# Fixed places for the backward fills and another order of heads in the paired DeltaNet scan

## The chip, the cores and the metric

One core of one Trainium2 chip. The time is the device time of one execution in microseconds (us); for before there are three runs and one profiled execution. An effect under about 0.2% (5 us) can't be told from no change here.

## What is computed

One layer of a hybrid backbone over 128 context tokens and 2048 latent tokens, width 1024. A normed and modulated input goes through one combined projection; half of its width feeds a gated DeltaNet with 4 heads of 128 in both directions, the other half a gated MLP; one output projection joins them, then comes a squared-ReLU MLP. The part that the change touches is the DeltaNet scan. Cut to its core:

```python
def step(S, xs):
    qd, kd, u_c, w_c, qk_c, gl = xs
    v_new = u_c - w_c @ S
    o = qd @ S + qk_c @ v_new
    S = S * exp(gl) + kd.T @ v_new
    return S, o
# u_c, w_c come from a triangular solve of (I + strict_lower(k_beta k^T * decay)) per chunk and head
out = concat([rmsnorm(o_f + flip(o_b)) * silu(gate), o_mlp]) @ w_out
```

## The kernel before

The program has three stages: the projections (up to about 457 us), the scan (457 to 1262 us), and the wide MLP. Instructions are issued in the order of a list of events, and the framework's scheduler then orders each engine's queue within the dependencies it is given. Every queue runs in order.

**Units and pairs.** The scan works on chunks of 128 tokens, `unit(t, d)` (d = 0 forward, 1 backward). There are 34 units, taken in pairs: the two context units first, then 16 forward units, then 16 backward ones. A pair inverts its two triangular matrices together, 8 heads at once (heads 0 to 3 are the first chunk's, 4 to 7 the second's), in fp16. These are the "prep" steps of `pair`: X is turned for each chunk (`turn`, L1143: four products on TensorE, then the copy Y on ScalarE); five levels, w = 2 to 32, each of two steps (`level`, L1157 to L1192); a last level at half size (L1206, L1218, L1222) and the refinement (L1234 to L1236) up to T (L1243, evicted by ScalarE at L1247). In a level the first step multiplies AH by Y for all heads (L1167), and VectorE copies the masked result into P (L1170); the second step multiplies P with X twice (L1181, L1187), and ScalarE copies the results back into Y and X (L1190). So a level goes TensorE, VectorE, TensorE, ScalarE, and each of these hands over to the next.

**The chain.** Each unit has four scan steps ("chain"): S by kT (L991) with vt on VectorE (L1049); vt by T (L991) with the copy vn on ScalarE (L1057); vn by kt (L991) with the new S on VectorE (L1079); and the output o (L1090, L1091; eviction L1094 to L1102). The next unit needs S.

**Fills.** Everything else in this stage is put between: the gMLP's projections while the forward units run, and in the backward part the output projection of finished tiles: gate and norm of o (L1385 to L1397), its transposes (`trans`, L1410), their two-part evictions oH on ScalarE (L1414) and oL on VectorE (L1415), 48 products per tile (L219 to L221), and the residual (L1434, L1435). For four of the tiles, operands of the MLP are prepared too (opH on ScalarE L873, opL on VectorE L874, stored by DMA L876).

**What sets the order.** Every event has a time in units of one chunk; `WINDOWS` (L57, L58) gives the windows: entries 2 and 3 are the chain's window of a unit, for forward (entries 0 to 7) and backward (8 to 17); entries 4 and 5 of the backward half are when norm, scaling and the two transposes of a unit are due, entries 6 and 7 its output projection, entries 8 and 9 the MLP's operands. `emit` adds ordering edges: a fill's first product on TensorE stands behind the newest chain or prep step but `lag`:

```python
elif pe and len(hist) > lag:
    tc.add_manual_dep(pe[0], hist[-1 - lag].name, ...)
for time, _, f, kind in sorted(events, key=lambda e: e[:2]):
    emit(f, kind, LAG2 if time < NT + 1 else LAG3)
```

`LAG2` is 0 and `LAG3` is 3. A three-product group L219, L220, L221 is one 128-row part of a product in split precision; a fill piece in this stage is two of them, six matmuls.

Of the kernel before, what the change touches and what calls it, by code (L numbers as in the profile page):

```python
# [24 lines left out]
H = 4  # L25
# [6 lines left out]
def interleave(*lists):  # L32
# [5 lines left out]
    for _, _, _, s in sorted(order, key=lambda e: e[:3]):  # L38
# [3 lines left out]
MOD_STEPS = (1, 1, 0, 0, 0, 1, 0, 2, 0, 1, 1, 2)  # L42
NS = 4
LAG2 = 0
LAG3 = 3
NF = 5
LATE = 0.1
PARTS = ((0, 2), (2, 4), (4, 6), (6, 8))
# [5 lines left out]
NK = DFF // P // 2  # L54
AHEAD = 3
COMPUTE = (mybir.EngineType.DVE, mybir.EngineType.Activation, mybir.EngineType.Pool)
WINDOWS = [2.0, 0.0, -0.225, 0.775, -2.1, 18.9, 17.58, 18.3,  # L57
           2.0, 0.0, -0.225, 0.775, 1.22, 1.5, 1.6875, 2.6875, 3.17, 3.71]  # L58


@with_exitstack
def hybrid_step(
# [7 lines left out]
    V, A, G, T = nc.vector, nc.scalar, nc.gpsimd, nc.tensor  # L70
# [12 lines left out]
    def f32(ap):  # L83
        return ap.bitcast(F32)
# [195 lines left out]
    with ExitStack() as ph:  # L280
# [478 lines left out]
        for bi in range(len(BLOCKS)):  # L759
# [8 lines left out]
            for n, (gi, h) in enumerate(order):  # L768
                u = us[n] if bi == 0 and n < 3 else feature_tile(blk, bi, gi, h)
# [156 lines left out]
    with ExitStack() as ph:  # L926
# [48 lines left out]
        def first_pe(fn):  # L975

            start = len(tc.nc.cur_bb.bb.instructions)
            fn()
            return [x.name for x in tc.nc.cur_bb.bb.instructions[start:] if x.engine == mybir.EngineType.PE][0]

        def unit(t, d, last=False):

            u = {}
# [5 lines left out]
            def quad(p, lhs, rhs):  # L989
                for h in range(H):  # L990
                    T.matmul(p[:, h, :], lhs[:, h, :], rhs[:, h, :], start=True, stop=True)  # L991
# [60 lines left out]
            @scan.append  # L1052
            def _():
                p = pd()
                pe = first_pe(lambda: quad(p, u["T"], u["vt"]))
                u["vn"] = q32("vn", 1)
                A.copy(u["vn"], p)  # L1057
                if not last:
                    behind(lambda: [A.activation(u["kt"][:, h, :], u["kt"][:, h, :], AF.Copy, scale=col(eglg, h))
                                    for h in range(H)], pe)  # L1060
                u["pe"] = pe
# [51 lines left out]
        def pair(us):  # L1113
# [3 lines left out]
            spans = [(0, 8, ds[0])] if ds[0] == ds[1] else [(0, 4, ds[0]), (4, 8, ds[1])]  # L1117
# [41 lines left out]
            def level(w):  # L1159

                @steps.append
                def _():
                    p = packed(pd8(), w)
                    for lo, hi, d in spans:
                        y = half(g["Y"], 1 - d, w)
                        for h in range(lo, hi):
                            T.matmul(p[:, h], g["AH"][:, h, :], y[:, h], start=True, stop=True)  # L1167
                    for lo, hi, d in spans:
                        mask = om[w].unsqueeze(1).to_broadcast([P, hi - lo, P]).bitcast(U16)
                        V.copy_predicated(out=half(pms[w][:, lo:hi], 1 - d, w), mask=half(mask, 1 - d, w),  # L1170
                                          data=p[:, lo:hi])

                @steps.append
                def _():
                    py, px = packed(pd8(), w), packed(pd8(), w)

                    def first():
                        for lo, hi, d in spans:
                            pm = half(pms[w], 1 - d, w)
                            for h in range(lo, hi):  # L1180
                                T.matmul(py[:, h], g["X"][:, h, :], pm[:, h], start=True, stop=True)  # L1181

                    pe = first_pe(first)
                    for lo, hi, d in spans:
                        x = half(g["X"], d, w)
                        for h in range(lo, hi):
                            T.matmul(px[:, h], pms[w][:, h, :], x[:, h], start=True, stop=True)  # L1187
                    for nm, p in (("Y", py), ("X", px)):
                        for lo, hi, d in spans:
                            A.copy(half(g[nm][:, lo:hi], 1 - d if nm == "Y" else d, w), p[:, lo:hi])  # L1190
                    if w == 2:
                        behind(lows, pe)  # L1192
# [180 lines left out]
        def o_steps(du):  # L1373
            t = du["t"]
            out = []
            u = {}

            def norm():
                du["ob"] = w512("ob")
                load(out=du["ob"], in_=ob_d[t * P : (t + 1) * P, :])  # L1380
                o, ga = du["o"], du["ga"]
                ss = smp.tile([P, 4], F32, tag="oss", name="oss")
                junk = fp.tile([P, P], BF16, tag="junk", name="junk", bufs=1)
                for h in range(H):
                    A.activation(junk, o[:, h, :], AF.Square, accum_out=ss[:, h : h + 1])  # L1385
                r2 = smp.tile([P, 4], F32, tag="r2", name="r2")
                rr = smp.tile([P, 4], F32, tag="rr", name="rr")
                V.tensor_tensor(out=r2, in0=rq[:, t, :], in1=rq[:, t, :], op=ALU.mult)
                V.tensor_tensor(out=r2, in0=r2, in1=ss, op=ALU.mult)
                rsqrt_cols(rr, r2, 4, 1.0 / P, EPS)  # L1390
                u["rr"] = rr

            def scaled():
                o, ga, rr = du["o"], du["ga"], u["rr"]
                V.scalar_tensor_tensor(out=rr, in0=rr, scalar=0.5, in1=rq[:, t, :], op0=ALU.mult, op1=ALU.mult)
                for h in range(H):
                    V.scalar_tensor_tensor(out=o[:, h, :], in0=o[:, h, :], scalar=rr[:, h : h + 1],  # L1397
                                           in1=ga[:, h * P : (h + 1) * P], op0=ALU.mult, op1=ALU.mult)

            def trans(half):  # L1400
                def f():
                    if half == 0:
                        u["H"], u["L"] = [], []
                        u["x"] = [w512("x"), w512("x")]
                        for n in range(2):
                            load(out=u["x"][n], in_=xrow(t)[:, n * 512 : (n + 1) * 512])
                    src = du["o"] if half == 0 else du["ob"].rearrange("p (h d) -> p h d", h=H)
                    ps = pj().rearrange("p (h d) -> p h d", h=H)
                    for h in range(H):
                        T.transpose(ps[:, h, :], src[:, h, :], ident)  # L1410
                    hs = hp.tile([P, 4, P], F32R, tag="h", name="oH")
                    ls = hp.tile([P, 4, P], F32R, tag="h", name="oL")
                    scale = 0.5 if half else vec[:, 68:69]
                    A.activation(hs, ps, AF.Copy, scale=scale)  # L1414
                    V.scalar_tensor_tensor(out=ls, in0=ps, scalar=scale, in1=f32(hs), op0=ALU.mult, op1=ALU.subtract)  # L1415
                    u["H"] += [hs[:, i, :] for i in range(4)]
                    u["L"] += [ls[:, i, :] for i in range(4)]
                return f

            def proj(n, k0):  # L1420
                def f():
                    if k0 == 0:
                        u["ps"] = pj()
                    for k in (k0, k0 + 1):
                        mm3(u["ps"], [(u["H"][k], u["L"][k]) + WO[n][k]], first=k == 0,
                            last=k == KT - 1)
                    if k0 == KT - 2:
                        sl = slice(n * 512, (n + 1) * 512)
                        tmp = fp.tile([P, 512], F32, tag="ug" if n else "vg", name="tmp")
                        ga = ga1[n]  # L1430
                        if cond(t) == 0:
                            ga = wrow(mod_d[0:1, 2 * D + n * 512 : 2 * D + n * 512 + 512])
                        x = u["x"][n]
                        V.tensor_tensor(out=tmp, in0=u["ps"], in1=ga, op=ALU.mult)  # L1434
                        V.tensor_tensor(out=x, in0=x, in1=tmp, op=ALU.add)  # L1435
                        du["x2"] = u["x"]
                        store(out=x2_d[t * P : (t + 1) * P, sl], in_=x)
                return f

            for n in range(2):  # L1440
                for k0 in range(0, KT, 2):
                    out.append(proj(n, k0))
            return [(0.0, norm, "fill"), (0.45, scaled, None), (0.7, trans(0), "fill"), (0.95, trans(1), "fill")], out
# [29 lines left out]

        p2, p3 = WINDOWS[:8], WINDOWS[8:]
        for i, u in enumerate(units):
# [91 lines left out]
        for time, _, f, kind in sorted(events, key=lambda e: e[:2]):  # L1567
            emit(f, kind, LAG2 if time < NT + 1 else LAG3)

# [396 lines left out]
    for j, t in enumerate(range(8, -1, -1)):  # L1966
        st = h2_steps(t, bank, lambda: junk16, w512, own=own_tile if t == 0 else None)
        p = 16 + 19 * j // 2
# [4 lines left out]
    for p, (o, n, m) in enumerate(seq):  # L1973
        u = units[n]
# [32 lines left out]
    for m, (n, i, u, q) in enumerate(todo):  # L2007
# [12 lines left out]
        h, lo = sops.pop(m)  # L2020
# [71 lines left out]
```

## Time and profile before

| | us |
|---|---|
| median of three runs (2613.26 to 2618.33) | 2614.32 |
| the profiled execution, by its own time | 2617.11 |
| its span, first to last instruction | 2615.1 |
| TensorE busy in the span | 2557.1 |
| scan stage, by the first and last instructions of it | 457 to 1262 |

In the rows of a timeline the columns are start in us, duration in us, engine, line, operation, out<-in, shapes, count, and in brackets the idle time of the engine before it and what ended it. A matmul with fp32 operands runs as two records, so that L991's four products show as x8. `pj`, `pm` and `pd` are PSUM tiles.

### The profile page before, as it was taken

To read this page: it belongs to the slowest core of one execution; us is meant where nothing else is said; L and a number is where in the kernel's file an instruction comes from. 1 tells how busy PE (TensorE), PEld (TensorE's weight loads), DVE (VectorE), ACT (ScalarE), POOL (GpSimd) and SP (SyncE) were. 2 spreads that over 40 slices of the span, in tenths; PEclk is the share of its full clock that TensorE was granted. 3 is DMA by queue.
4 is the path that set the end of the run, shared out by engine and by line. 5 is a ranking of instruction groups with operands and counts; after the bars stand their busy time and mean duration, and the time that the engine had idled before them with its cause. 6 is when DMAs were issued, how large, how long until landed. Compare 5 with 4: busy or idle time off the path is not lost.

```text
span 2615.1 us, 43888 instructions
## 1 busy us (share of the span) xinstructions
PE 2557.1 (98%) x15330; PEld 2144.0 (82%) x15330; DVE 1759.1 (67%) x3490; ACT 1223.6 (47%) x2894; POOL 265.4 (10%) x478
## 2 busy tenths in 40 slices
PE   8999999899999999999999999999999999999998
PEld 4899999687888877778888888888887888888887
DVE  5777746656667767786488786677675544775874
ACT  4755555555555657674255653333342432332441
POOL 3112112111212122221000000000000000000000
PEclk9999999999999999999999999999999999999999
DMA  8866637755555757896678789545369978786773
GB/s 285 292 221 211 195 119 235 232 151 152 165 165 173 219 184 232 262 292 196 268 228 244 242 253 318 150 126 162 107 208 376 332 266 287 260 254 213 229 259 105
DMA packets 533859, 579.77 MB, mean 222 GB/s; under 512 B 35500, under 2 KB 366684, under 8 KB 530054
## 3 DMA queue, kind: packets, MB, share of 16 engines
q1 hardware_dynamic: 533638, 576.98, 69.2%
q8 instruction: 120, 1.97, 0.3%
q14 instruction: 101, 0.83, 0.1%
HBM read 397.62 MB, written 179.22 MB: 221 GB/s over the span
## 4 chain that ended last, share of the span: by engine, by line
PE 57%; DMA 3%; DVE 2%; ACT 1%; issue 1%; SPq 0%; DVEq 0%; POOLq 0%; ACTq 0%
PE f L219 16%; PE f L221 16%; PE f L220 16%; PE pj L221 1%; PE pj L219 1%; PE pj L220 1%; PE pd L991 1%; DMA r<-in_w_ff_dram 1%; PE pm L219 1%; PE pm L221 1%; PE pm L220 1%; DMA t_d<-r 1%; DMA traw<-in_w_ff_dram 0%; PE pd L1090 0%; PE pd L1091 0%
## 5 line engine op out<-in xcount | busy, mean ns | idle before, releaser
L219 PE MATMUL f<-hop,zH 128*128 128x512 f32 x960 | 373.8, 390 | 2.1 <-ACT zH L1595 2.1
L221 PE MATMUL f<-hop,zL 128*128 128x512 f32 x960 | 373.9, 390 | 0.0
L220 PE MATMUL f<-hop,zH 128*128 128x512 f32 x960 | 373.2, 389 | 0.0
L219 PE MATMUL f<-hop,wH 128*128 128x512 f32 x896 | 351.5, 393 | 0.2 <-ACT wH L1742 0.2
L220 PE MATMUL f<-hop,wH 128*128 128x512 f32 x896 | 348.9, 390 | 0.0
L221 PE MATMUL f<-hop,wL 128*128 128x512 f32 x896 | 344.0, 390 | 0.0
L1595 ACT CAST zH<-zraw 128x512 fp32r<-128x512 f32 x240 | 146.7, 620 | 295.1 <-DVE zraw L1589 86.2
L219 PEld LDWEIGHTS f<-hop,zH 128*128 128x128 f32 x960 | 180.2, 188 | 40.9 <-ACT zH L1595 3.9
L221 PEld LDWEIGHTS f<-hop,zL 128*128 128x128 f32 x960 | 180.2, 188 | 39.9 <-DVE zL L1589 2.7
L220 PEld LDWEIGHTS f<-hop,zH 128*128 128x128 f32 x960 | 180.2, 188 | 37.2
L1589 DVE TENSOR_TENSOR zL<-zraw,zH 128x512 fp32r<-128x512 f32 x240 | 162.4, 687 | 71.1 <-ACT zH L1595 55.3
L221 PEld LDWEIGHTS f<-hop,wL 128*128 128x128 f32 x896 | 168.2, 188 | 35.7
L219 PEld LDWEIGHTS f<-hop,wH 128*128 128x128 f32 x896 | 168.5, 188 | 34.5 <-issue 0.9
L220 PEld LDWEIGHTS f<-hop,wH 128*128 128x128 f32 x896 | 168.5, 188 | 32.2
L221 PE MATMUL pj<-kH,wL 128*128 128x386 f32 (+2 forms) x568 | 190.9, 336 | 0.0
L220 PE MATMUL pj<-kL,wH 128*128 128x386 f32 (+2 forms) x568 | 189.7, 334 | 0.0
L219 PE MATMUL pj<-kH,wH 128*128 128x386 f32 (+2 forms) x568 | 189.2, 336 | 0.3 <-DVE kH L486 0.3
L177 POOL TENSOR_TENSOR r<-rsq,nhalf 128x1 f32<-128x1 f32 (+1 forms) x38 | 22.9, 603 | 1357.9 <-DVE rsq L176 1357.9
L1742 ACT CAST wH<-s 128x512 fp32r<-128x512 f32 x96 | 58.9, 620 | 170.9 <-DVE s L1589 157.5
L536 DVE SCALAR_TENSOR_TENSOR cv<-pj,vec,cv 128x384 f32<-128x384 f32 (+2 forms) x164 | 87.1, 539 | 57.1 <-ACT cv L533 55.7
L219 PEld LDWEIGHTS pj<-kH,wH 128*128 128x128 f32 x568 | 107.2, 189 | 4.6 <-issue 4.2
L221 PEld LDWEIGHTS pj<-kH,wL 128*128 128x128 f32 x568 | 107.7, 190 | 0.5
(409 smaller groups left out, 5728.7 us busy)
## 6 DMA issues: line engine op xcount, KB each, us to landing
zraw<-z_d SPq DMA_DIRECT2D x212, 256.0 KB, 4.4
raw<-in_w_ff_dram SPq DMA_DIRECT2D x128, 256.0 KB, 4.7
hop<-hop_d SPq DMA_DIRECT2D x28, 1024.0 KB, 16.5
z_d<-c SPq DMA_DIRECT2D x96, 256.0 KB, 2.5
zraw<-s_d SPq DMA_DIRECT2D x96, 256.0 KB, 4.7
raw<-in_w_mod_dram SPq DMA_DIRECT2D x80, 256.0 KB, 4.3
r<-in_w_ff_dram SPq DMA_DIRECT2D x80, 256.0 KB, 5.3
s_d<-s SPq DMA_DIRECT2D x64, 256.0 KB, 3.0
```

Of the source, the lines that this page charges most:

```text
L177: G.tensor_tensor(out=out, in0=t[:np_, :n], in1=nhalf[:np_, :n], op=ALU.pow)
L219: T.matmul(ps, lh, rh, start=first and i == 0, stop=False, skip_group_check=more)
L220: T.matmul(ps, lh, rl, start=False, stop=False, skip_group_check=more)
L221: T.matmul(ps, ll, rh, start=False, stop=last and i == n - 1, skip_group_check=more)
L536: V.scalar_tensor_tensor(out=cv[:, o : o + m], in0=ps[:, s + sh : s + sh + m], scalar=convw[:, w, j : j + 1], in1=cv[:, o : o + m], op0=AL ...
L991: T.matmul(p[:, h, :], lhs[:, h, :], rhs[:, h, :], start=True, stop=True)
L1589: V.tensor_tensor(out=out, in0=a, in1=b, op=op)
L1595: A.copy(h, src)
L1742: A.copy(h, s2)
```

## The change

Five edits, none of which adds or removes an operation (both programs have the same number of instructions of each kind on each engine):

- `LAG3` from 3 to 0: in the backward part a fill stands behind the newest chain or prep step, as it does in the forward part already.
- The chain's window is 0.095 units later in both directions (-0.225 to 0.775 becomes -0.13 to 0.87), so that its four steps come at other places between the prep steps; norm to transposes in the backward part are due 0.07 to 0.05 units earlier.
- The four heads of the product vt by T are written last head first.
- The eight heads of a level's first step are written last head first, so that the first product reads the second chunk's Y.
- The transposes of `trans` are written last head first.

```diff
-LAG3 = 3
+LAG3 = 0
...
-WINDOWS = [2.0, 0.0, -0.225, 0.775, -2.1, 18.9, 17.58, 18.3,
-           2.0, 0.0, -0.225, 0.775, 1.22, 1.5, 1.6875, 2.6875, 3.17, 3.71]
+WINDOWS = [2.0, 0.0, -0.13, 0.87, -2.1, 18.9, 17.58, 18.3,
+           2.0, 0.0, -0.13, 0.87, 1.15, 1.45, 1.6875, 2.6875, 3.17, 3.71]
...
                 p = pd()
-                pe = first_pe(lambda: quad(p, u["T"], u["vt"]))
+                pe = first_pe(lambda: [T.matmul(p[:, h, :], u["T"][:, h, :], u["vt"][:, h, :], start=True, stop=True)
+                                       for h in reversed(range(H))])
...
                     p = packed(pd8(), w)
-                    for lo, hi, d in spans:
+                    for lo, hi, d in reversed(spans):
                         y = half(g["Y"], 1 - d, w)
-                        for h in range(lo, hi):
+                        for h in reversed(range(lo, hi)):
                             T.matmul(p[:, h], g["AH"][:, h, :], y[:, h], start=True, stop=True)
...
-                    for h in range(H):
+                    for h in reversed(range(H)):
                         T.transpose(ps[:, h, :], src[:, h, :], ident)
```

From line 1056 on, the changed kernel's lines stand one further down (L1167 is L1168 there, L1181 is L1182, L1410 is L1411, L1415 is L1416; vt by T is L1055).

**First place, TensorE: the first level (w = 2) of the fourth pair, forward.** `pd_7735` is the level's first product, `P2_5732` its masked copy, `vn_7715` and `kt_7355` belong to the chain. Before:

```order
L1167 MATMUL pd_7735<-Y_7674,AH_7624 128x64
L219 MATMUL pj_7745<-wH_5395,hH_7462 128x512
L220 MATMUL pj_7745<-wL_5396,hH_7462 128x512
...
L221 MATMUL pj_7745<-wH_5407,hL_7466 128x512
L991 MATMUL pd_7759<-vn_7715,kt_7355 128x128 x4
L1167 MATMUL pd_7735<-Y_7674,AH_7624 128x64
L1181 MATMUL pd_7767<-P2_5732,X_7673 128x64
```

After:

```order
L1055 MATMUL pd_7722<-vt_7357,T0_7630 128x128 x4
...
L1168 MATMUL pd_7735<-Y_7674,AH_7613 128x64
L219 MATMUL pj_7745<-wH_5395,hH_7462 128x512
L220 MATMUL pj_7745<-wL_5396,hH_7462 128x512
...
L221 MATMUL pj_7745<-wH_5407,hL_7466 128x512
L1182 MATMUL pd_7759<-P2_5732,X_7673 128x64
```

Before, the level's eight products are split, four ahead of a fill piece and four behind it and behind the chain's vn by kt, and the products that read P follow with nothing between. After, the eight stand together, a fill piece of six stands behind them, and vn by kt is no longer there.

**Second place, VectorE, the same level.** Rows around the masked copy P2. Before:

```order
L1269 TENSOR_TENSOR gw_7752<-pj_7606,gw_7752 128x512
L1079 TENSOR_TENSOR S_7764<-pd_7759,se_7613 128x512
L1170 COPY_PREDICATED P2_5732<-om2_186,pd_7735 128x256x2
L1274 SCALAR_TENSOR_TENSOR ug_7757<-gw_7752,pj_7606 128x512
L1157 TENSOR_TENSOR AL_7625<-KK_7224,AH_7624 128x512
```

After:

```order
L176 TENSOR_SCALAR rsq_7691<-mv_7677 128x4
L1269 TENSOR_TENSOR gw_7752<-pj_7606,gw_7752 128x512
L1171 COPY_PREDICATED P2_5732<-om2_186,pd_7735 128x256x2
L1314 TENSOR_SCALAR vg_7622<-vg_7622,mv_7677,rs_7690 128x128 x4
L1270 TENSOR_TENSOR gw_7752<-pj_7606,gw_7752 128x512
L1158 TENSOR_TENSOR AL_7614<-KK_7224,AH_7613 128x512
```

The new state S stood ahead of the masked copy and has left this place.

**Third place, TensorE, the end of a backward pair.** `pm_14394` before and `pm_14375` after are the transposes of the same tile, `oH` and `oL` their evictions, `pj_14531` the output projection that reads them. Before:

```order
L1410 MATMUL pm_14394<-ident_173,o_14127 128x128 x3
...
L1206 MATMUL pd_14466<-Y_13926,AH_13879 64x64
...
L219 MATMUL pj_14531<-wH_11462,oH_14399 128x512
L220 MATMUL pj_14531<-wL_11463,oH_14399 128x512
...
L1222 MATMUL pd_14499<-X_13925,R_14467 64x64
L221 MATMUL pj_14531<-wH_11462,oL_14400 128x512
```

After:

```order
L1411 MATMUL pm_14375<-ident_173,o_14163 128x128 x4
L1411 MATMUL pm_14395<-ident_173,ob_14288 128x128 x4
...
L991 MATMUL pd_14442<-vn_14341,kt_13919 128x128 x4
L219 MATMUL pj_14347<-wH_12015,oH_14046 128x512
...
L1207 MATMUL pd_14466<-Y_13926,AH_13868 64x64
...
L219 MATMUL pj_14347<-wH_12102,oH_14046 128x512
...
L1219 MATMUL pd_14487<-R_14467,X_13925 64x64
...
L221 MATMUL pj_14531<-wH_11462,oL_14381 128x512
```

Before, between the transposes and the first product that reads oL stand the small products L1206, the output products and two matmuls of the same projection. After, twelve matmuls of the tile before (`pj_14347`) and vn by kt stand there too, and the products L1206 and L1218 are six fills apart (there L1207 and L1219).

## The prediction

> **What bounds the kernel now.** I read the page first, then busy time by stage, then TensorE's waits, then the timeline around the longest of them. The page's line for TensorE, and the scan cut into its first pair, the forward pairs and the backward part:
>
> ```profile
> PE 2557.1 (98%) x15330; PEld 2144.0 (82%) x15330; DVE 1759.1 (67%) x3490; ACT 1223.6 (47%) x2894; POOL 265.4 (10%) x478
> 457.00:505.00 48.00, 40.29 (x309) 30.33 (x308) 27.54 (x72) 25.98 (x65) 9.97 (x12) 1.00 0.74 245
> 505.00:921.00 416.00, 405.22 (x3520) 337.59 (x3520) 277.51 (x723) 228.70 (x539) 80.49 (x90) 1.00 0.58 173
> 921.00:1262.00 341.00, 323.35 (x2739) 265.54 (x2738) 242.10 (x542) 203.78 (x570) 65.03 (x73) 0.99 0.74 234
> ```
>
> The columns are the stretch, its length, busy time of TensorE, its weight loads, VectorE, ScalarE and GpSimd, the granted clock, the DMA share and GB/s. TensorE is the bound everywhere, so the change, which leaves its work alone, can only win what TensorE loses by waiting in the scan: 7.7, 10.8 and 17.6 us in the three stretches, 36.1 us in all. Here is what it waited for, over the whole program (total us, times, longest) and then in the first pair alone (460 to 505 us):
>
> ```profile
> PE pd L1181 <- DVE P L1170: 17.1, 21, 1.6
> PE pj L221 <- DVE oL L1415: 8.4, 5, 2.0
> ...
> PE pd L1143 <- DVE X L1135: 4.0, 7, 1.1
> PE pd L1167 <- ACT Y L1190: 3.7, 9, 0.5
> ```
>
> ```profile
> PE pd L1181 <- DVE P L1170: 3.7, 5, 1.6
> PE pd L1167 <- ACT Y L1190: 1.5, 4, 0.4
> PE pd L1143 <- DVE X L1135: 1.1, 1, 1.1
> PE pd L1234 <- ACT Y L1225: 0.5, 1, 0.5
> PE pd L1218 <- ACT R L1209: 0.5, 1, 0.5
> PE pd L1206 <- ACT Y L1190: 0.3, 1, 0.3
> ```
>
> All four large ones are hand-overs inside the scan: 33.2 us in 42 waits. None is for a DMA.
>
> **Split levels.** The wait for P at the change's first place, TensorE and then VectorE:
>
> ```profile
> 597.08 0.48 PE L219 MATMUL pj<-wH,hH 128*128 128x512 f32 x1
> 597.39 0.39 PE L220 MATMUL pj<-wL,hH 128*128 128x512 f32 x1
> 597.62 0.40 PE L221 MATMUL pj<-wH,hL 128*128 128x512 f32 x1
> ...
> 598.55 1.05 PE L991 MATMUL pd<-vn,kt 128*128 128x128 f32 x8
> 599.44 0.28 PE L1167 MATMUL pd<-Y,AH 128*128 128x64 f16 x4
> 601.02 0.40 PE L1181 MATMUL pd<-P,X 128*128 128x64 f16 x8 [1.30 <-DVE P L1170]
> ```
>
> ```profile
> 599.64 0.69 DVE L1079 TENSOR_TENSOR S<-pd,se 128x512 f32<-128x512 f32 x1 [0.71 <-PE pd L991]
> 600.25 0.72 DVE L1170 CAST_PREDICATED P<-om,pd 128x512 f16<-128x512 uint16 x1
> ```
>
> Six fills take 1.47 us (597.08 to 598.55) and stand where they cover nothing; then the second half of the level comes, and its reader follows at once. VectorE, whose queue has S first, delivers P at 600.97, 1.53 us after the level's last products began. After the change the eight products stand together and the six fills behind them. By this trace the P copy alone takes 0.72 us from then on, so 1.47 us cover it, and S, which is made by vn by kt, no longer stands ahead of it. The page of waits shows idle time only. A wait costs more: a fill is busy for 0.39 us but the next starts 0.23 us after it (597.39, 597.62), so 0.16 us of overlap is lost each time.
>
> What of this comes back after the change? The cover of every level is one fill piece. Where VectorE has other work in hand, that is too little, as here, in the backward part:
>
> ```profile
> 959.44 0.28 PE L1167 MATMUL pd<-Y,AH 128*128 128x64 f16 x4
> ```
>
> ```profile
> 960.08 0.68 DVE L1079 TENSOR_TENSOR S<-pd,se 128x512 f32<-128x512 f32 x1
> 960.68 0.72 DVE L1170 CAST_PREDICATED P<-om,pd 128x512 f16<-128x512 uint16 x1
> ```
>
> P ends at 961.40, 1.96 us after 959.44. Against 0.12 us for the four products and 1.47 for six fills, 0.4 us would be left, 0.56 with the lost overlap. If that meets as many levels as wait now, 21, it is 12 us; if none, nothing. No row says which, as VectorE is 71% busy there (242 of 341 us), so I take the middle, 6.
>
> **oL and the backward fills.** The third place:
>
> ```profile
> 1074.83 0.62 PE L1410 MATMUL pm<-ident,o 128*128 128x128 f32 x3
> 1075.38 0.43 PE L1206 MATMUL pd<-Y,AH 64*64 64x64 f16 x8
> ...
> 1081.28 0.80 PE L221 MATMUL pj<-wH,oL 128*128 128x512 f32 x1 [2.04 <-DVE oL L1415]
> ```
>
> ```profile
> 1080.48 0.74 DVE L1415 SCALAR_TENSOR_TENSOR oL<-pm,vec,oH 128x512 fp32r<-128x512 f32 x1
> ```
>
> ```profile
> 1077.95 0.58 ACT L1209 CAST R<-pd 64x512 f16<-64x512 f32 x1
> ```
>
> The projection of a tile begins before its oL is there: oL, which waits for its turn on VectorE, comes 6.4 us after the transposes (1074.83 to 1081.22). With `LAG3` = 0 the projection stays at its place, behind the steps that now stand between; there two pieces of the tile before (2.9 us) and vn by kt (0.9, 598.55 to 599.44) come in addition to the output products, which cover the same in both. So about 3.8 us more cover stands against a wait of 2.04. I count the 8.4 us as gone.
>
> Moving the fills out has a price: between L1206 and L1218 stood the output products (and a pair of fills); now six fills, 1.47 us. The cast R that they wait for ended at 1078.53, 3.15 us after L1206 began, because ScalarE's queue was full. With 1.6 us of cover that would be a wait of 1.55, or 1.7 with the lost overlap, in each of the eight backward pairs: at most 14 us; at least nothing, where ScalarE is free. I take 7.
>
> **X and Y.** The turn's first product stood right behind T; by the chain's shift S by kT and a fill piece now come between, and the wait (4.0 us) is gone except at the scan's entry (1.1). Of the waits for Y (3.7), those of the first pair stay: its two chunks run in opposite directions, and the second half of a level still stands directly ahead of the next. With L1234, L1218 and L1206 there, 3.9 us stay. The reversed heads of vt by T and of the transposes issue the same products; their readers wait for all four heads anyway. I cost them at nothing, and the fill piece that stands ahead of them covers that; without it the price would be a wait like the longest of the list's, 1.6 us, per unit. SP, with its loads, and GpSimd get the same work in a similar order; no row above waits for a DMA.
>
> **The clock.** Right after the wait at 1081.28 the granted clock (third figure from the right) was 0.50, after an equal wait it was not:
>
> ```profile
> 1081.00:1084.00 3.00, 2.72 (x9) 2.25 (x9) 3.00 (x6) 1.44 (x7) 0.69 (x2) 0.50 0.84 241
> 1128.00:1131.00 3.00, 1.28 (x7) 1.05 (x8) 3.00 (x7) 2.82 (x10) 1.61 (x2) 1.00 0.98 292
> 1081.87 0.63 PE L219 MATMUL pj<-wH,oH 128*128 128x512 f32 x1
> 1082.30 0.63 PE L220 MATMUL pj<-wL,oH 128*128 128x512 f32 x1
> ```
>
> Matmuls came 0.43 us apart there instead of 0.23, so some 2.8 us ran at half speed: 1.4 us, which I count as won. [...]
>
> **The sum.** Idle time in the scan 36.1, less 3.9 that stays: 32.2. Lost overlap at 37 of the 42 large waits (five of the first pair's stay), 0.16 each: 5.9. Clock: 1.4. That is 39.5 us at most. Less 6 and 7 for waits that come anew: 26.5 us. The profiled execution took 2617.1 us, so it would take 2590.6; it stood 2.8 us over the median of 2614.3, and against that I forecast 2587.8, in round figures 2588. With nothing new it is 2575, with both new waits at their upper ends (12 and 14) 13.5 us are left: 2601.
>
> **Rivals.** *Half of it only*: the backward part wins nothing, since VectorE is full there and oL, P and R change places in being late. Then the first pair's P waits and the forward ones are left, about 10.8 + 3.8 of idle time, less 1 that stays and 3 of new waits, 11 us: 2603. For it: VectorE took 6.4 us to deliver oL, for an operation of 0.74. Against: it is oL's reader that moves away. Chance 0.08.
>
> *No change*: P late by 0.5 us at nearly all 85 levels, 43 us, which eats the whole gain: 2614 give or take 5. For it: the cover is one piece everywhere, where most levels now have two or a chain step. Against: P alone needs half of it. Chance 0.05.
>
> *Slower*: the casts opH stand in ScalarE's queue and wait for the store of an earlier one:
>
> ```profile
> 1073.53 4.06 DMA hop_d<-opH
> ```
>
> ```profile
> ACT opH L873 <- DMA hop_d<-opH: 2.4, 2, 2.2
> ```
>
> With fills held, TensorE has one piece (1.47) between a step and its reader, and if an opH with a store of 4.06 us ahead of it stands before the Y or R of that step, 2.6 us are lost. There are 28 such casts for the high parts (four tiles, seven operands each): 73 us if all, 2588 + 73 = 2661; it turns slower from the eleventh on, and with half of them it is 2624. Against: ScalarE waited for such a store twice, 2.4 us in all. Chance 0.05.
>
> **How the numbers follow.** The forecast has 0.82 and is faster throughout; half of it only is faster too. About 0.2% (5 us) is what can be told from no change: faster 0.90, same 0.05, slower 0.05. The range goes from 2575, all of it, over the forecast's upper end of 2601 to the half gain with 2 us to spare, 2605; outside lie the no-change and slower cases and a little of the ends.
>
> **What would show it.** Right: TensorE's idle time between 457 and the scan's end near 1236 falls from 36 to some 15 us; the wait of L221 for oL is gone from the list; P's is down from 17 us to 6 or so, in many short waits; the clock is 1.00 in the backward part. The steps are wrong singly if waits of L1219 for R exceed 14 us (ScalarE decides), if P's wait total stays near 17 (the cover is too short), or if X waits stay at 4. The whole is wrong if the scan's length is within 5 us of 805 us, or if idle time falls but the matmuls' spacing grows.

## The result, and the profile after

The changed kernel takes 2587.38 us (median of 4 runs, 2585.80 to 2591.70), the kernel before 2616.32 us in runs beside it (median of 4, 2613.26 to 2620.03): the ratio is 0.9891 with an interval of 0.9872 to 0.9911, 28.9 us less. The forecast was 2588.

The page's line for TensorE of the changed kernel, and then its scan in the three stretches of the prediction, their ends taken at the same instructions (first pair, forward pairs, backward part; after the length come TensorE, its weight loads, VectorE, ScalarE, GpSimd, the granted clock, DMA share and GB/s):

```profile
PE 2548.7 (99%) x15330; PEld 2136.1 (83%) x15330; DVE 1759.1 (68%) x3490; ACT 1228.2 (48%) x2894; POOL 262.7 (10%) x478
```

```profile
453.30:498.20 44.90, 39.75 (x310) 30.12 (x309) 28.91 (x72) 25.76 (x65) 10.77 (x12) 1.00 0.80 261
498.20:900.30 402.10, 398.84 (x3492) 329.39 (x3492) 272.44 (x707) 227.67 (x530) 74.71 (x88) 1.00 0.57 177
900.30:1231.30 331.00, 323.77 (x2771) 268.53 (x2770) 246.01 (x558) 209.99 (x580) 67.52 (x74) 1.00 0.75 244
```

Length less busy time gives 5.15, 3.26 and 7.23 us of idle time, 15.6 in all where there were 36.1. The three stretches together are 778.0 us long, 27.0 less than the 805.0 of before. So 20.5 us of the gain is idle time, and 6.5 is what the idle time does not show: overlap of consecutive matmuls (at 596.35 us of the changed kernel a fill is busy for 0.39 us and the next starts 0.23 us after it), and the clock, which is 1.00 in every stretch of this execution (before lost 1.4 us at the fall in its scan). The profiled execution took 2585.8 us, 31.3 less than the one before; the 4.3 us beyond the scan lie mostly in the first stage, which the change leaves alone and which took 460 to 466 us in the traces of this study. For that reason the experiments below are compared by the length of the scan; the two traces of the changed kernel agree in it to 0.8 us. Each other length is from one trace, so a difference of 1 us is not told from none.

What TensorE waited for in the changed kernel over the whole program (total us, times, longest):

```profile
PE pd L1168 <- ACT Y L1191: 4.4, 4, 1.6
...
PE pm L1411 <- DVE o L1398: 3.5, 4, 1.1
PE pd L1182 <- DVE P L1171: 2.8, 5, 1.1
...
PE pm L1411 <- DMA ob<-ob_d: 1.6, 1, 1.6
PE pd L1144 <- DVE X L1136: 1.5, 2, 0.9
PE pd L1219 <- ACT R L1210: 0.8, 2, 0.5
...
PE pj L221 <- DVE oL L1416: 0.3, 1, 0.3
```

P is down from 17.1 us to 2.8, oL from 8.4 to 0.3, X from 4.0 to 1.5. Y, at 4.4 (3.7 before), is now the largest. Two rows are new: the transposes (L1411) wait for o and, once, for ob. Here is the prediction's first place after the change, TensorE and then VectorE:

```profile
588.50 0.40 PE L1168 MATMUL pd<-Y,AH 128*128 128x64 f16 x8
588.73 0.47 PE L219 MATMUL pj<-wH,hH 128*128 128x512 f32 x1
...
589.97 0.40 PE L221 MATMUL pj<-wH,hL 128*128 128x512 f32 x1
590.21 0.41 PE L1182 MATMUL pd<-P,X 128*128 128x64 f16 x8
```

```profile
588.98 0.74 DVE L1171 CAST_PREDICATED P<-om,pd 128x512 f16<-128x512 uint16 x1
```

The eight products stand together, P is done at 589.72, and six fills later, at 590.21, its reader starts without a wait.

### The profile page after: what moved, and what is told of

Same layout as the page of the kernel before. It is cut to its first block, busy times and chain, and to the rows that moved or that the text cites. A ratio compares the mean times of both kernels' runs of the same rounds, so it can differ in the third digit from the quotient of the medians.

```text
span 2584.1 us, 43895 instructions
## 1 busy us (share of the span) xinstructions
PE 2548.7 (99%) x15330; PEld 2136.1 (83%) x15330; DVE 1759.1 (68%) x3490; ACT 1228.2 (48%) x2894; POOL 262.7 (10%) x478
## 4 chain that ended last, share of the span: by engine, by line
PE 52%; DMA 3%; DVE 1%; issue 1%; ACT 0%; SPq 0%; DVEq 0%; POOLq 0%; POOL 0%; ACTq 0%
PE f L219 15%; PE f L220 15%; PE f L221 15%; DMA r<-in_w_ff_dram 1%; PE pj L219 1%; PE pj L221 1%; PE pj L220 1%; DMA t_d<-r 1%; PE pd L991 0%; PE f L855 0%; PE pd L1091 0%; PE pd L1092 0%; DVE hop L1590 0%; DMA x<-x_d 0%; DMA zraw<-z_d 0%
## 5 line engine op out<-in xcount | busy, mean ns | idle before, releaser
L219 PEld LDWEIGHTS f<-hop,zH 128*128 128x128 f32 x960 | 180.2, 188 | 40.7 <-ACT zH L1596 3.8
L220 PEld LDWEIGHTS f<-hop,wH 128*128 128x128 f32 x896 | 168.5, 188 | 32.2
L220 PEld LDWEIGHTS pj<-kL,wH 128*128 128x128 f32 x568 | 107.4, 189 | 0.5
```

Of the source, the lines that this page charges most:

```text
L219: T.matmul(ps, lh, rh, start=first and i == 0, stop=False, skip_group_check=more)
L220: T.matmul(ps, lh, rl, start=False, stop=False, skip_group_check=more)
```

## The experiments

Each kernel is before or the changed kernel with an edit. Scan lengths are between the same instructions, from the traces: *first* is pair 1, from its first turn product to that of pair 2; *forward* is pairs 2 to 9; *backward* is pairs 10 to 17 and the rest up to the first product of the MLP. Waits are TensorE's, in us.

| kernel | median us | ratio's interval | first | forward | backward | scan | P | X | oL | o, ob |
|---|---|---|---|---|---|---|---|---|---|---|
| before | 2616.3 | | 43.2 | 349.8 | 416.5 | 809.5 | 17.1 | 4.0 | 8.4 | |
| changed | 2587.4 | 0.9872 to 0.9911 | 40.0 | 340.0 | 402.1 | 782.2 | 2.8 | 1.5 | 0.3 | 5.1 |
| e1 level heads alone | 2602.7 | 0.9935 to 0.9960 | 42.0 | 341.7 | 415.7 | 799.5 | 0.2 | 4.3 | 9.7 | |
| e2 held fills alone | 2600.6 | 0.9925 to 0.9950 | 43.2 | 349.8 | 405.6 | 798.6 | 18.6 | 4.7 | | 0.8 |
| e3 windows alone | 2596.2 | 0.9909 to 0.9936 | 43.4 | 346.4 | 402.6 | 792.4 | 13.5 | 2.4 | 2.7 | |
| e4 all but windows | 2582.0 | 0.9857 to 0.9884 | 40.7 | 341.7 | 398.8 | 781.2 | 0.3 | 5.8 | 0.3 | 0.6 |
| e5 changed again | 2587.2 | 0.9865 to 0.9901 | 40.4 | 340.0 | 402.6 | 783.0 | 1.9 | 1.7 | 0.3 | 4.5 |
| e6 forward windows only | 2583.9 | 0.9849 to 0.9890 | 39.9 | 340.0 | 397.9 | 777.8 | 0.3 | 3.3 | 0.3 | 0.6 |
| e7 transposes due as before | 2587.8 | 0.9866 to 0.9907 | 40.3 | 340.0 | 403.0 | 783.2 | 6.9 | 2.6 | 0.3 | 1.8 |
| e8 all but held fills | 2587.7 | 0.9863 to 0.9902 | 40.3 | 340.0 | 401.9 | 782.2 | 2.7 | 2.4 | 4.5 | |
| e9 all but level heads | 2598.4 | 0.9923 to 0.9948 | 43.4 | 346.8 | 404.8 | 795.0 | 12.2 | 1.5 | 0.3 | 4.6 |
| e10 all but vt, transposes | 2586.1 | 0.9874 to 0.9900 | 40.7 | 340.0 | 401.2 | 782.0 | 2.8 | 1.6 | | 1.4 |
| e11 e6, transposes in order | 2580.0 | 0.9847 to 0.9876 | 40.4 | 340.0 | 395.2 | 775.7 | 0.6 | 3.1 | | |
| e12 backward: due times only | 2581.6 | 0.9855 to 0.9882 | 40.9 | 340.0 | 396.8 | 777.7 | 1.4 | 1.3 | 0.3 | |

An empty field means that the list has no such wait. The column before "first" is the 95% interval of the ratio to runs of the kernel before on the same chip (their medians: 2616.0 to 2617.2 us). Against before, every kernel gains more by the runs than by the scan, 1.6 to 5.7 us. Before's runs beside the experiments had a granted clock of 0.997 on the mean, the traced one 0.998 (0.001 of 2616 us is 2.6 us): this one trace probably lost less to the clock than most executions, so that the gains in scan length over before are some 3 us low. Differences among the other kernels are not touched by this.

**e1, the reversed level heads alone.** To before:

```diff
-                    for lo, hi, d in spans:
+                    for lo, hi, d in reversed(spans):
                         y = half(g["Y"], 1 - d, w)
-                        for h in range(lo, hi):
+                        for h in reversed(range(lo, hi)):
```

> Only the reversed heads of the levels' first step. Theory (each edit removes one kind of wait, and the parts add): all levels stand as eight products, the 17.1 us of idle time at P fall to some 3, the waits for oL, X and Y stay; with the lost overlap 14 to 18 us faster than before. Rival (VectorE is the limit in the backward part, so only the forward pairs win): the forward waits for P go (8 us with the first pair's), the backward ones stay or turn up elsewhere: 6 to 10 us faster.

The run took 2602.74 us against 2616.04, ratio 0.9947. P's waits are gone, all but 0.2 us, and with them 8.0 us of the forward pairs; the backward part gave nearly nothing, 0.8 us. TensorE's largest waits inside the scan:

```profile
PE pj L221 <- DVE oL L1415: 9.3, 5, 2.0
PE pd L1167 <- ACT Y L1190: 5.4, 8, 2.0
...
PE pd L1143 <- DVE X L1135: 4.3, 7, 1.4
```

The waits for oL are as long as before, but here they cost more than themselves. TensorE after one of them, and then, soon after it, 3.3 us with their granted clock (third figure from the right, 0.51):

```profile
1021.01 0.50 PE L221 MATMUL pj<-wH,oL 128*128 128x512 f32 x1 [2.03 <-DVE oL L1415]
...
1023.53 0.63 PE L221 MATMUL pj<-wH,oL 128*128 128x512 f32 x1
1023.96 0.63 PE L219 MATMUL pj<-wH,oH 128*128 128x512 f32 x1
```

```profile
1022.40:1025.70 3.30, 3.30 (x11) 2.59 (x9) 1.93 (x7) 1.51 (x4) 1.45 (x2) 0.51 0.74 206
```

The granted clock fell to a half five times in this run's scan, for 3.4 us each, 1.7 us lost each time; before had one such fall, which cost 1.4 us, since half a microsecond of it lay in the wait. The 7.1 us more can account for what the run lacks to the 14 to 18 us of the theory: 10.0 in the scan and 7.1 make 17.1. By the runs it is 13.3 us faster, between the theory and the rival. That only the forward pairs win is as the rival had it, but not for its reason: the backward waits for P are gone too. TensorE's idle time in the backward part fell by 4.9 us, from 20.1 to 15.2, and its four falls cost 5.4 more than the one of before.

**e2, held fills alone.** To before:

```diff
-LAG3 = 3
+LAG3 = 0
```

> Only the backward fills held behind the newest step. Theory: the waits for oL and oH (9.3 us) go, P, X and Y stay; 8 to 12 us faster. Rival (oL, P and R change places in being late): within 4 us of before, with P's or R's waits in the backward part up by what oL's lose.

2600.59 us, ratio 0.9937, the scan 10.9 us shorter, all of it in the backward part. By the runs it is 15.5 us faster, more than the 8 to 12 expected. The waits for oL are gone, as predicted; those for P and X stay:

```profile
PE pd L1181 <- DVE P L1170: 18.6, 26, 1.6
PE pd L1143 <- DVE X L1135: 4.7, 10, 0.8
```

**e3, the windows alone.** To before (the whole edit of `WINDOWS`):

```diff
-WINDOWS = [2.0, 0.0, -0.225, 0.775, -2.1, 18.9, 17.58, 18.3,
-           2.0, 0.0, -0.225, 0.775, 1.22, 1.5, 1.6875, 2.6875, 3.17, 3.71]
+WINDOWS = [2.0, 0.0, -0.13, 0.87, -2.1, 18.9, 17.58, 18.3,
+           2.0, 0.0, -0.13, 0.87, 1.15, 1.45, 1.6875, 2.6875, 3.17, 3.71]
```

> Only the shifted windows. Theory: the waits for X (4.0 us, 2.9 of it inside) and part of those for Y go, P's and oL's stay; 4 to 7 us faster. Rival (the chain's place is what makes P late, since S stands ahead of it): P's waits fall by more than half too, and 12 us or more are won.

2596.16 us, ratio 0.9922, the scan 17.1 us shorter, 19.9 by the runs. The theory's size fell. The rival's size was right, but not its reason: P's waits fell by a fifth, from 17.1 to 13.5 us, not by more than half. In the backward part the windows alone give 13.9 us, more than the held fills; they shorten oL's wait as well, to 2.7 us:

```profile
PE pd L1181 <- DVE P L1170: 13.5, 20, 1.5
...
PE pj L221 <- DVE oL L1415: 2.2, 4, 0.7
...
PE pm L221 <- DVE oL L1415: 0.5, 2, 0.3
```

The three edits alone shorten the scan by 10.0, 10.9 and 17.1 us, 38.0 together, and the whole change by 27.3. They remove in part the same waits, and, as e4 to e12 show, the windows cost time in the backward part once the other edits are there.

**e4, all but the windows.** The changed kernel with `WINDOWS` of before.

```diff
-           2.0, 0.0, -0.13, 0.87, 1.15, 1.45, 1.6875, 2.6875, 3.17, 3.71]
+           2.0, 0.0, -0.225, 0.775, 1.22, 1.5, 1.6875, 2.6875, 3.17, 3.71]
```

(with -0.225, 0.775 in the line ahead too)

> All edits but the shifted windows. Theory: the waits for P and oL go, those for X stay (some 4 us and the lost overlap); 4 to 7 us slower than the changed kernel, 22 to 25 faster than before. Rival (chain's place): P stays late, at most 16 us faster than before.

2582.01 us, ratio 0.9871 (0.9857 to 0.9884). That expectation was wrong: the kernel is not slower than the changed one. The forward pairs are 1.6 us longer, as X waits again, but the backward part is 3.4 us shorter. TensorE's two largest waits:

```profile
PE pd L1168 <- ACT Y L1191: 5.9, 4, 2.3
PE pd L1144 <- DVE X L1136: 5.8, 10, 1.9
```

**e5 and e6, the changed kernel again, and with the windows of before in the backward part only.** e5 has no edit; e6 has, to the changed kernel, only the line shown under e4.

> The changed kernel itself, as the measure for the other three. Both theories: 0.987 to 0.991 of before; the scan stage 782 us long, 27 less than before.

> The changed kernel with the backward windows as they were before. Theory: the shift helps the forward pairs (no wait for X) and costs the backward ones (transposes that wait for o, 3.5 us; pairs 13 to 15 take 44.4 us against 43.4 without the shift), so this is 3 to 6 us faster than the changed kernel. Rival: the waits for X come back in the backward pairs and eat that: within 2 us of it.

e5 took 2587.19 us, as expected, and e6 2583.91 us; the intervals of their ratios, 0.9865 to 0.9901 and 0.9849 to 0.9890, overlap, but the scan is 4.4 to 5.2 us shorter in e6, nearly all of it in the backward part, as the theory had it; the waits for X come back in part (3.3 us, 1.5 and 1.7 in the two traces of the changed kernel). e5, the changed kernel itself, had one fall of the clock in its scan, after a wait of 1.91 us for Y in pair 11:

```profile
899.97:903.37 3.40, 3.23 (x23) 2.37 (x22) 3.05 (x7) 1.94 (x4) 1.04 (x1) 0.50 0.95 348
```

**e7 and e12, which half of the backward windows costs.** e7 keeps the chain's shift and takes the due times of norm and transposes as before; e12 does the opposite. To the changed kernel:

```diff
-           2.0, 0.0, -0.13, 0.87, 1.15, 1.45, 1.6875, 2.6875, 3.17, 3.71]
+           2.0, 0.0, -0.13, 0.87, 1.22, 1.5, 1.6875, 2.6875, 3.17, 3.71]
```

```diff
-           2.0, 0.0, -0.13, 0.87, 1.15, 1.45, 1.6875, 2.6875, 3.17, 3.71]
+           2.0, 0.0, -0.225, 0.775, 1.15, 1.45, 1.6875, 2.6875, 3.17, 3.71]
```

> The changed kernel with norm and transposes due as before, the chain's windows shifted. If the earlier transposes make the waits for o: those 3.5 us go and the backward pairs 13 to 15 fall to some 43.5 us, 2 to 4 us faster than the changed kernel. If the chain's shift makes them (o is later by as much): they stay, within 2 us.

> The changed kernel with the backward part's chain where it was before; of the backward windows only the earlier due times of the norm and the transposes stay. Theory (what costs time in the backward part is the chain's shift, by which the cover of P falls from two fill pieces to one, and not the due times): pairs 13 to 15 take 43.4 us as with the windows of the forward part alone, pair 11 takes under 50 us, TensorE waits for P under 2 us, and the scan is 3 to 5 us shorter than the changed kernel's. Rival (the due times cost it): the scan is within 1.5 us of the changed kernel's and pair 11 stays at 51 to 52 us.

With e5 and e6 this is a square. Backward part with the chain shifted: 402.1 and 402.6 us (due times early), 403.0 (as before). With the chain in its old place: 396.8 (early), 397.9 (as before). The shift costs 5 to 6 us there. The due times give 0.4 to 1.1 us, which is not clear of noise: e4 and e6 have the same windows in the backward part and differ by 0.9. e7 took 2587.82 us: the waits for o fell to 0.5 us, so the earlier due times have a part in them, but pairs 13 to 15 took 44.6 us and nothing was won, as P was waited for instead. e12 came out as its theory had it: 43.5 us for pairs 13 to 15, and a scan 4.5 to 5.3 us shorter than the changed kernel's. e7's first row of waits and e12's for P:

```profile
PE pd L1182 <- DVE P L1171: 6.9, 8, 1.4
```

```profile
PE pd L1182 <- DVE P L1171: 1.4, 3, 0.5
```

Pair 11, where the forward fills end and the backward ones begin, shows how. In the changed kernel it takes 51.95 us (48.49 before), with 5.4 us idle; in e12 48.26. TensorE and VectorE at one of its levels in the changed kernel:

```profile
895.72 0.40 PE L1168 MATMUL pd<-Y,AH 128*128 128x64 f16 x8 [1.42 <-ACT Y L1191]
...
897.19 0.40 PE L221 MATMUL pm<-wH,hL 128*128 128x512 f32 x1
898.69 0.40 PE L1182 MATMUL pd<-P,X 128*128 128x64 f16 x8 [1.10 <-DVE P L1171]
```

```profile
897.32 0.69 DVE L1080 TENSOR_TENSOR S<-pd,se 128x512 f32<-128x512 f32 x1
897.92 0.72 DVE L1171 CAST_PREDICATED P<-om,pd 128x512 f16<-128x512 uint16 x1
```

S stands ahead of P again, as it did at the first place before the change, and the cover is one fill piece. The same level in e6, with the chain in its old place:

```profile
899.12 0.39 PE L221 MATMUL pm<-wH,hL 128*128 128x512 f32 x1
899.35 0.38 PE L1091 MATMUL pd<-S,qT 128*128 128x128 f32 x2
...
900.91 0.39 PE L1092 MATMUL pd<-vn,QK 128*128 128x128 f32 x2
901.13 0.40 PE L1182 MATMUL pd<-P,X 128*128 128x64 f16 x8
```

There the output products (899.35 to 901.13, 1.8 us) stand behind the fill piece, and P is no longer waited for.

**e8, all but the held fills.** The changed kernel with `LAG3 = 3`.

```diff
-LAG3 = 0
+LAG3 = 3
```

> All edits but the held fills. Theory (a held fill is what frees oL): the waits for oL and oH return, 9 us and their lost overlap, 8 to 12 us slower than the changed kernel. Rival (the windows alone free oL, as they left 2.7 us of its 8.4): at most 4 us slower.

2587.68 us, ratio 0.9883 (0.9863 to 0.9902), the scan 782.2 us: the same as the changed kernel. Some of oL's wait comes back, 4.5 us, and the transposes' waits for o go:

```profile
PE pj L221 <- DVE oL L1416: 3.1, 6, 0.9
...
PE pm L219 <- DVE oL L1416: 1.4, 1, 1.4
```

The theory fell, the rival was right: next to the windows the held fills gain no time that can be told. They do remove those 4.5 us, but the waits for o and ob, 5.1 us, stand in their place.

**e9, all but the level heads.** The changed kernel without the edit that e1 makes.

```diff
-                    for lo, hi, d in reversed(spans):
+                    for lo, hi, d in spans:
                         y = half(g["Y"], 1 - d, w)
-                        for h in reversed(range(lo, hi)):
+                        for h in range(lo, hi):
```

> The changed kernel, but the level's first step takes its heads in the order of before, so that again 42 level halves of four products stand apart in the scan. Theory (the reversed heads are what removes the late P, since they keep a level's eight products together): TensorE's waits for P come back to 13 to 17 us, the scan is 8 to 12 us longer than the changed kernel's, and the run takes 8 to 12 us more than it. Rival (the places of the chain and the held fills relieve P as well, so that the reversed heads add little on top): P's waits stay under 8 us and the run is within 4 us of the changed kernel.

2598.43 us, ratio 0.9936 (0.9923 to 0.9948). The scan is 12.8 us longer than the changed kernel's, with 3.4 in the first pair, 6.8 in the forward pairs and 2.7 in the backward part. P is back:

```profile
PE pd L1182 <- DVE P L1171: 12.2, 19, 1.4
```

The theory holds; its figure for P was a little high, that for the scan a little low. This edit has no substitute among the others.

**e10 and e11, the transposes in order.** e10 is the changed kernel with vt by T and the transposes as before; e11 is e6 with the transposes as before. The edit of the transposes, which both have (e10 also takes back the lines of vt by T that the change's diff shows):

```diff
-                    for h in reversed(range(H)):
+                    for h in range(H):
                         T.transpose(ps[:, h, :], src[:, h, :], ident)
```

> The changed kernel, but vt by T and the transposes take their heads in the order of before. Theory (these two edits issue the same products and are worth nothing by themselves, but the transposes, which begin with the head that is made last, wait 3.5 us in all for o): the waits of the transposes for o fall below 2 us, pairs 13 to 15 are up to 0.5 us shorter each, and the run is within 3 us of the changed kernel. Rival (the reversed order of vt by T relieves the waits for T or for vt): new waits of that product appear and the run is over 4 us longer.

> The changed kernel with the windows of the backward part as before and the transposes' heads in the order of before. Theory (the backward windows cost 3 to 5 us in the scan and the reversed transposes under 1 us): the scan is 4 to 6 us shorter than the changed kernel's, the waits of TensorE for P are under 2 us, those for X 2 to 4 us, and the run takes 2580 to 2584 us. Rival (the gain of the forward windows alone was chance): the scan is within 2 us of the changed kernel's.

In the changed kernel o is scaled head by head on VectorE, and the transposes begin with the head that comes last. TensorE and VectorE in pair 13:

```profile
1004.18 0.39 PE L221 MATMUL pj<-wH,oL 128*128 128x512 f32 x1
1005.65 0.66 PE L1411 MATMUL pm<-ident,o 128*128 128x128 f32 x4 [1.08 <-DVE o L1398]
1006.14 0.60 PE L1411 MATMUL pm<-ident,ob 128*128 128x128 f32 x4
1006.58 0.40 PE L1182 MATMUL pd<-P,X 128*128 128x64 f16 x8
```

```profile
1003.26 2.33 DVE L1398 SCALAR_TENSOR_TENSOR o<-o,rr,ga 128x128 f32<-128x128 f32 x4
1005.51 0.68 DVE L1171 CAST_PREDICATED P<-om,pd 128x512 f16<-128x512 uint16 x1
```

The same place in e10:

```profile
1007.41 0.39 PE L221 MATMUL pj<-wH,oL 128*128 128x512 f32 x1
1007.64 0.27 PE L1410 MATMUL pm<-ident,o 128*128 128x128 f32 x1
1007.75 0.60 PE L1410 MATMUL pm<-ident,ob 128*128 128x128 f32 x4
1008.19 1.01 PE L1410 MATMUL pm<-ident,o 128*128 128x128 f32 x3
1009.46 0.39 PE L1181 MATMUL pd<-P,X 128*128 128x64 f16 x8 [0.27 <-DVE P L1170]
```

With the heads in order the first transpose fits at once, those of ob come next, and the other three follow as their heads come. Pairs 13 to 15 take 43.92 us on the mean, 44.37 in the changed kernel. The run as a whole takes 2586.12 us, within 1.3 us of the changed kernel, as the theory said. Waits for o of 3.4 us and more occur only where the order is reversed, the chain shifted, the transposes due early and the fills held (the changed kernel, e5, e9). Without the reversed order (e10), the shift (e12) or the held fills (e8) there are 0.2 us or none, with the later due times (e7) 0.5. The edit of vt by T was never tried by itself, but transposes run only in the backward part, so that in the forward pairs it is all that e10 leaves out: 340.0 us with it and without it.

e11 took 2580.00 us, ratio 0.9861 (0.9847 to 0.9876), the fastest of all: its scan is 6.5 us shorter than the changed kernel's and 2.1 shorter than e6's, of which e6's wait for o explains 0.6; the rest stays open. The run and P's and X's waits came out as its theory had them, the scan a little better (6.5 us for 4 to 6). By the scan it beats both kernels; by the times its interval just touches those of the changed kernel (from 0.9872, and from 0.9865 in e5).

## Why the prediction was right, point by point

**The bound and the size.** TensorE was the bound, its work stayed as it was, and the gain is what it lost by waiting: the scan became 27.0 us shorter in the profiled execution where 26.5 were forecast. That this is so close is partly luck, since terms erred in both directions. I left 16.9 us of idle time (36.1 less 32.2, and 13 new); 15.6 are there, but other ones: first pair 5.15, P 2.8, o 3.5, ob 1.6, Y in pair 11 1.4, and 1.2 in small waits.

**P.** The step was right: what removes the 17 us is that the eight products stand together (e1: P 0.2; e9: P 12.2). The term for new waits was 6 us; it measured 2.8, in five waits. My row with S ahead of P and 0.4 us left over was of the right kind, but such levels are few: two waits of over 1 us in pair 11 and three of 0.2.

**R.** Taken as 7 us (at most 14), measured 0.8, of which 0.5 was there before. The mis-sized term is the delay in ScalarE's queue. At the place that I quoted R ended 3.15 us after L1206 began, and in pairs 12 to 15 of before it was 3.15 to 3.26 everywhere. In the changed kernel it is 2.00 us in pairs 13 to 15, 2.30 in pair 16 (which waits 0.3) and 1.05 to 1.31 in the other backward pairs. In pair 13, TensorE and then ScalarE:

```profile
1009.51 0.43 PE L1207 MATMUL pd<-Y,AH 64*64 64x64 f16 x8
...
1011.56 0.31 PE L1219 MATMUL pd<-R,X 64*64 64x64 f16 x5
```

```profile
1010.93 0.58 ACT L1210 CAST R<-pd 64x512 f16<-64x512 f32 x1
```

R is done at 1011.51, and its reader starts at 1011.56, when the six fills end: the cover just suffices there, with nothing to spare. That the queue would be shorter was not foreseen, so that the small cost is in part luck.

**oL.** The forecast, 8.4 us gone, held. The reason given, that with `LAG3` = 0 the projection stays at its place, is one of two ways: it suffices (e2), but the windows alone leave only 2.7 us of it (e3), and next to them it gains no time (e8). This step claimed more than the trace of before could show.

**X, Y and the first pair.** X fell to 1.5 us, by the windows as predicted (e4, without them: 5.8); in the backward part the earlier due times alone do nearly as well as the chain's shift (e12: 1.3 in all, e6 without either: 3.3). In the first pair 5.15 us stayed, not 3.9: P went, but Y's wait rose from 1.5 to 2.9 us. That is a price of the reversed level heads: each of the ten traces with them has a wait for Y of 1.4 to 2.5 us in the first pair, and none of the four without them has one over 0.9.

**What I costed at nothing.** For vt by T it was right (e10's forward pairs). For the transposes it was wrong. I argued that the readers wait for all four heads anyway and that a fill piece covers the start; but the transposes themselves read o head by head, and reversed they wait for the last one: 3.5 us. That no row of the scan waits for a DMA was true of before; in the changed kernel one does, 1.6 us for ob, in pair 11. And I saw no loss in the chain's shift, which costs 5 to 6 us in the backward part (the changed kernel against e12, e7 against e6); it was hidden in the sum by the waits that did not come.

**Clock and lost overlap.** Put at 1.4 and 5.9 us, 7.3 together; 6.5 is what the scan gained beyond idle time. The clock is 1.00 throughout the changed kernel's scan in the execution compared, but not in all: e5, the same kernel, had one fall. So that part of the term is luck of the execution. e1 shows that it could have decided: with four falls in its backward part that kernel's time there fell by 0.8 us only.

**The rivals.** Half of it only: no, the backward part gained 14.4 us. No change (P late everywhere): no, five waits. Slower (opH casts behind a store): ScalarE waited for such a store once, 2.7 us.

## What to carry to other kernels

Where two hand-overs alternate, keep the products of one step together and put the filler whole between step and reader; a step that was split around its filler had no cover here, and no other edit replaced that. Edits that free the same wait don't add up, so try each alone and each left out: the backward half of this change's windows cost 4 to 5 us of the scan, more than the forward half won (1.6 us in the forward pairs). When an order of heads is reversed, look at who produces the operand head by head, not only at who reads the result.

## What the runs showed of the hardware

In these traces a stall of about 2 us cost TensorE either 2 us or nearly 4, and its length did not decide which. In the scans of all fourteen traces there were 20 idle gaps of 1.8 to 2.5 us; at eight of them the granted clock went to 0.50 for 3.4 us (1.4 to 1.7 us lost), beginning 0.55 us before the restart in before, 0.6 us after it in e5 and 1.3 us after it in e10. Gaps of 2.30 us (e4) and 2.47 us (e12) left it at 1.00, one of 1.91 us (in e5) did not, and one fall (in e8) came after a gap of 1.38 us. Before had one fall at three such gaps, of 2.03 and 2.04 us, e1 five at five, with a mean granted clock of 0.996 over the execution.

What decides at which gap the clock falls is not shown. In the trace of before it is 0.50 from 87.45 to 90.86 us, in the first stage, and from 1080.73 to 1084.14: both times for 3.413 us, and the second fall begins 993.28 us after the first, 291 times that. No gap in these scans was over 2.5 us.

Beside this, the first stage took 459.5 to 465.6 us in these traces, while the forward pairs come out at 340.0 us in all eight that have the level heads and the forward windows.
